# Hybrid decoder trunk on one core: retention's gated read-outs turned to channel rows by VectorE and a trip through DRAM on ScalarE's queue, in place of TensorE transposes

## The chip, the cores and the metric

One core of one Trainium2 chip. The time is device microseconds of the one program that the kernel launches; the median of three runs before the change is 1691.69 us. The core has five engines that run side by side, each with its own queue of instructions taken in order: TensorE (PE; PEld is its weight load), VectorE (DVE), ScalarE (ACT), GpSimd (POOL) and SyncE (SP), which only issues transfers. ACT and POOL issue transfers too, from the same queue as their computing. Engines wait for each other by semaphores; an instruction that waits holds all that stands behind it on its engine.

## The reference, cut to what matters

Two layers over 512 tokens of 1024 channels. Each layer mixes three branches of 512 channels (RWKV-7, retention, spatial gating), merges them by gates, and ends in a gated MLP. Of retention and the merge:

```python
y = (inner + cross).transpose(0, 2, 3, 1, 4).reshape(B, S, RET_HEADS, RET_V_DIM)
y = y * lax.rsqrt(jnp.mean(y * y, axis=-1, keepdims=True) + EPS)
return (y.reshape(B, S, RET_V_WIDTH) * jax.nn.silu(g)).astype(p.dtype)
...
branches = jnp.stack([y_rw, y_ret, y_sg], axis=2)
proj = jnp.einsum('bsgc,gcd->bsgd', branches, w_branch[l])
gates = jax.nn.sigmoid(gate_logits.reshape(B, S, N_BRANCH, D_MODEL))
x = x + jnp.sum(gates * proj, axis=2) @ w_out[l]
```

Retention has 4 heads with 128 value channels. Everything is float32 for the output's sake: a float32 product is made of three faster ones, with each operand split into a rounded high half and the low rest.

## The kernel before, in words

**Layout.** The merge wants a branch's output with channels on the partitions (128 channels by 512 tokens, one such tile per head). Retention is computed with tokens on the partitions: four chunks of 128 tokens, each a tile of 128 tokens by 512 channels, `yg[c]` (the trace and the order call these tiles vt). So `yg` has to be turned.

**Split products.** `mm3` (L157 inside it) makes one 128x128 by 128x512 product as three matmuls: low by high, high by high, high by low. `split` (L149, L150) makes the halves of an operand: a cast on ACT, then the difference on DVE. Weights go the same way: `load` (L127) brings 128x512 from DRAM on SP into one of three slots (wr), `part` (L140, L141) makes sh on ACT and sl on DVE. `unit` runs this ahead: in this stage, parts are written in the program three units before they are used. A load slot is free again when DVE has made its low half.

**Merges.** `merge(l, br, m, y)` loads a gate tile (gth) by a POOL transfer (L1071), makes one accumulator tile (acc, one of four in PSUM) with twelve matmuls from one unit, and empties it on DVE (L1074). Branch 0 is RWKV, 1 retention, 2 gating. Branch 2 adds to branch 0's tile on POOL (L1077), branch 1 on DVE, after which the sum is split. A fifth accumulator has to wait until the first of the four is emptied.

**Retention.** `ret_heads` prepares, `ret_pair` (matmuls at L948) is called three times: scores and states; read-outs of chunks 0 and 1 with scores of 2 and 3; read-outs of chunks 2 and 3, called the last pair below. A read-out is copied by ACT (L972), squared (L991), summed on DVE (L993, L994: rss), raised to -1/2 on POOL (L996: rrr), and multiplied into `yg` on DVE (L999, four products of 128x128 per chunk). `ret_out` (L1006) then transposes 16 blocks of 128x128 on TensorE into four PSUM tiles (sm), which `split` empties.

**Gating.** `sgu_out` (L1059) makes one of four blocks: four products into one sm tile, then DVE and a split.

**The order.** The string SEQ sets in which order `mixer` writes these steps into the program: 0, 1, 2 a merge of that branch; S a `ret_pair`; G a `sgu_out`; U units of gating's first factor; H `ret_heads`; Y `ret_out`. A scheduler then places the instructions on the engines by its own estimate of when each is ready, except those that are handed to `keep_in_program_order`, which stay in the order written. While `self.keep` is set, loads and parts of weights are among them. The matmuls of a merge are not pinned, so the scheduler may begin a merge, leave it for another and come back.

Of the kernel before, what the change touches and what calls it, by code (L numbers as in the profile page):

```python
# [8 lines left out]
F32 = mybir.dt.float32  # L9
F32R = mybir.dt.float32r  # L10
# [3 lines left out]
ADD, SUB, MUL, POW, MAX = ALU.add, ALU.subtract, ALU.mult, ALU.pow, ALU.max  # L14
# [3 lines left out]
S = 512  # L18
NC = 4
# [6 lines left out]
KEPT = 6  # L26
PRE = {(0, "f", 2): 0, (0, "f", 4): 1, (0, "f", 6): 2, (0, "f", 8): 3, (0, "d", 0): 4, (0, "d", 1): 5, (0, "d", 2): 6, (0, "d", 3): 7,
       (0, "d", 4): 8, (0, "d", 5): 9, (0, "d", 6): 10}
SEQ = "0 H G G 0 S 0 U U S G 0 G 0 0 S 2 2 Y 0 0 2 1 2 1 2 1 2 1 2 1 2 1 1 1"
NRAW = 3  # L30
AHEAD = {None: 2, "p": 4, "r": 3, "f": 3, "u": 5, "q": 4}
DEEP = 6
# [20 lines left out]
class Emit:  # L53
# [357 lines left out]
    def mixer(self, l, nst):  # L411
        self.pool = None
        with self.tc.tile_pool(name=f"rw{l}", bufs=1) as rp:
            self.rwp = rp
            self.filler = self.fillers(l)
            st = self.rwkv(l, nst)
        for _ in self.filler:
            pass
        self.rp = self.tc.tile_pool(name=f"ff{l}", bufs=NFP)
        self.fp = self.rp.__enter__()  # L420
        self.gup, self.bs, self.ws = self.f(n="gup"), self.f((128, 4, 128), n="bs"), self.f((128, 4, 128), n="ws")
        with self.tc.high_priority():
            self.nc.sync.dma_start(self.gup, self.a["gup"][l])
        self.nc.sync.dma_start(self.bs.rearrange("p g i -> p (g i)"), self.a["sgb"][l:l + 1, :].to_broadcast([128, 512]))
        self.nc.sync.dma_start(self.ws, self.a["sgw"][l])
        self.pool = "f"
        sg, out = self.sgu_v(l), self.rwkv_out(l, *st)
        self.nc.vector.tensor_tensor(self.ws, self.ws, self.c("le").unsqueeze(1).to_broadcast([128, 4, 128]), op=MUL)
        self.qk = []
        for c in range(NC):  # L430
            self.qk.append(self.f(n="qkT"))
            self.turned(self.qk[c], self.f(n="qkt"), self.ro[c], self.nc.gpsimd)
        self.wsp = self.split(self.ws.rearrange("p g i -> p (g i)"), self.f)
        for step in (sg, sg, out, sg, out, sg, None, out, sg, out, sg):
            next(step) if step else self.sgu_bias()
        yrw, ysg, mg, out, m2 = self.yrw, [], [], [], 0
        self.pool = "r"
        rest = self.sgu_u(l, range(2, 4))
        rows = iter([((), (0, 1), (0, 1, 2)), ((0, 1), (2, 3)), ((2, 3),)])
        for step in SEQ.split():  # L440
            if step == "S":
                self.ret_pair(*next(rows))
            elif step == "G":
                ysg.append(self.sgu_out(len(ysg)))
            elif step == "H":
                self.ret_heads()
            elif step == "U":
                next(rest), next(rest)
            elif step == "Y":
                yret = self.ret_out()  # L450
            elif step == "0":
                mg.append(self.merge(l, 0, len(mg), yrw))
            elif step == "2":
                mg[m2] = self.merge(l, 2, m2, ysg, mg[m2])
                m2 += 1
            else:
                out.append(self.split(self.merge(l, 1, len(out), yret, mg[len(out)], self.nc.vector), self.f))
        return out
# [398 lines left out]
    def ret_proj(self, l):  # L857
        nc, V, A, a = self.nc, self.nc.vector, self.nc.scalar, self.a
        g, tabs = self.supK(l, 14), []
# [5 lines left out]
        try:  # L865
            next(g)
        except StopIteration as e:
            pss = e.value
        self.ro, self.vt, self.yg, self.R, self.sc = [], [], [], {}, {}
        qs = [self.u(n="qs") for _ in pss]  # L870
        for c, ps in enumerate(pss):
            A.activation(qs[c], ps, AF.Identity, scale=self.rsT[:, c:c + 1])
# [3 lines left out]
        for i, out in ((18, self.vt), (22, self.yg)):  # L876
            g = self.supK(l, i)
# [8 lines left out]
            for c, ps in enumerate(pss):  # L886
                t = self.u(n="vt")
# [52 lines left out]
    def ret_pair(self, read=(), score=(), state=()):  # L940
# [47 lines left out]
        for k, c in enumerate(read):  # L988
# [8 lines left out]
            for i in range(4):  # L997
                o = g[:, 128 * i:128 * i + 128]
                V.scalar_tensor_tensor(o, y[:, i, :], rr[:, i:i + 1], o, op0=MUL, op1=MUL)  # L999

    def ret_out(self):
        out = []
        for h in range(4):
            pt = self.sm()
            for c in range(NC):
                self.tc.keep_in_program_order(self.nc.tensor.transpose(pt[:, c * 128:c * 128 + 128], self.yg[c][:, h * 128:h * 128 + 128], self.c("ident")))  # L1006
            out.append(self.split(pt, self.f))
        return out


    def sgu_v(self, l):
# [470 lines left out]
```

## Time and profile before

| what | value |
| --- | --- |
| median of three runs | 1691.69 us (1690.4 to 1692.12) |
| the profiled execution | 1690.56 us |
| its span, first to last instruction | 1688.9 us |
| mean granted TensorE clock | 0.999 of full |
| merges of layer 1, start of the first and last emptying (L1074) | 367.6 to 457.0 us of the span |
| the same of layer 2 | 1211.8 to 1301.2 us |

The span is what the profile divides into shares; the profiled execution's own time has 1.7 us around it. A row of the timeline has start, length, engine, line, operation and tiles, and in brackets how long the engine idled before it and for whom. A group row has count, then busy time in all, mean ns of one, and the idle time before it with its releaser. The chain of waits follows the program back from its last instruction, so its pieces have no gaps that another piece doesn't explain. Matmuls overlap: each lasts some 0.39 us, but the next begins sooner.

### The profile page before, as it was taken

What the parts mean: (1) busy time and instruction counts of PE and PEld (TensorE: products, weight loads), DVE (VectorE), ACT (ScalarE), POOL (GpSimd) and SP (SyncE); (2) the same over time, 40 slices, a digit from 0 to 9 for tenths busy, and PEclk for the clock granted to TensorE, in tenths of its full rate; (3) what the DMA queues carried; (4) which work ended last, traced back from release to release, by engine and by line L of the source; (5) the groups of instructions that cost most, each with busy time, mean ns of one, the idle gap of its engine ahead of it and who ended that gap; (6) DMA issues with size and microseconds to landing.
All of it is one profiled execution on the core that took longest, in us unless ns stands there. A gap on an engine that the chain in (4) does not pass through costs nothing.

```text
span 1688.9 us, 27943 instructions
## 1 busy us (share of the span) xinstructions
PE 1680.4 (100%) x10247; PEld 1382.5 (82%) x10247; DVE 1216.6 (72%) x2115; ACT 793.7 (47%) x1365; POOL 261.2 (15%) x376
## 2 busy tenths in 40 slices
PE   9999999999999999999999999999999999999998
PEld 7888877888888888888888888778888888888887
DVE  7888745578669887655568888455786688887777
ACT  6563543554255444433346544335542544444555
POOL 1121000303301200003321210003032012220000
PEclk9999999999999999999999999999999999999999
DMA  5236553625544532147743265536254424443775
GB/s 183 88 110 207 178 176 96 189 85 171 184 150 144 194 124 94 62 146 264 251 146 97 91 208 186 176 99 187 86 173 157 156 94 144 144 141 113 245 241 177
DMA packets 143385, 260.01 MB, mean 154 GB/s; under 512 B 19440, under 2 KB 35440, under 8 KB 143248
## 3 DMA queue, kind: packets, MB, share of 16 engines
q1 hardware_dynamic: 117056, 188.41, 34.7%
q0 software_dynamic: 17552, 54.15, 9.7%
q10 hardware_dynamic: 8640, 15.67, 2.6%
q8 instruction: 80, 1.31, 0.3%
q14 instruction: 57, 0.47, 0.1%
HBM read 212.94 MB, written 45.22 MB: 153 GB/s over the span
## 4 chain that ended last, share of the span: by engine, by line
PE 98%; DVE 1%; ACT 0%; issue 0%; DMA 0%; DVEq 0%; ACTq 0%
PE acc L157 89%; PE sm L157 3%; PE sm L696 2%; PE sm L948 1%; PE sm L603 1%; PE sm L1059 0%; PE acc L359 0%; PE sm L566 0%; PE sm L565 0%; PE sm L1006 0%; DVE wl L141 0%; PE sm L850 0%; PE acc L319 0%; PE sm L841 0%; DMA wr<-wall 0%
## 5 line engine op out<-in xcount | busy, mean ns | idle before, releaser
L157 PE MATMUL acc<-lo,sh 128*128 128x512 f32 x1108 | 432.9, 391 | 0.0
L157 PE MATMUL acc<-hi,sh 128*128 128x512 f32 x1108 | 431.6, 390 | 0.0
L157 PE MATMUL acc<-hi,sl 128*128 128x512 f32 x1108 | 425.2, 390 | 0.0
L140 ACT CAST sh<-wr 128x512 fp32r<-128x512 f32 (+1 forms) x375 | 226.5, 614 | 305.3 <-PE acc L157 163.8
L141 DVE TENSOR_TENSOR sl<-wr,sh 128x512 fp32r<-128x512 f32 (+1 forms) x375 | 253.2, 684 | 95.9 <-ACT sh L140 71.5
L141 DVE TENSOR_TENSOR wl<-wr,wh 128x512 fp32r<-128x512 f32 x238 | 168.2, 710 | 139.9 <-ACT wh L140 136.0
L140 ACT CAST wh<-wr 128x512 fp32r<-128x512 f32 x238 | 146.8, 619 | 246.6 <-PE acc L157 166.2
L157 PEld LDWEIGHTS acc<-lo,sh 128*128 128x128 f32 x1108 | 208.1, 188 | 43.9 <-issue 0.9
L157 PEld LDWEIGHTS acc<-hi,sl 128*128 128x128 f32 x1108 | 208.1, 188 | 43.4 <-issue 0.2
L157 PEld LDWEIGHTS acc<-hi,sh 128*128 128x128 f32 x1108 | 208.2, 188 | 42.5
L157 PE MATMUL acc<-lo,wh 128*128 128x512 f32 x584 | 230.2, 394 | 0.0
L157 PE MATMUL acc<-hi,wl 128*128 128x512 f32 x584 | 228.2, 391 | 0.0
L157 PE MATMUL acc<-hi,wh 128*128 128x512 f32 x584 | 227.9, 390 | 0.0
L1125 ACT ACTIVATE cv<-fu,pc 128x512 f32<-128x512 f32 x88 | 71.7, 816 | 134.6 <-DVE fu L1123 134.6
L157 PEld LDWEIGHTS acc<-lo,wh 128*128 128x128 f32 x584 | 109.7, 188 | 23.7 <-DVE rwp L525 0.3
L157 PEld LDWEIGHTS acc<-hi,wl 128*128 128x128 f32 x584 | 109.7, 188 | 23.7 <-issue 0.9
L157 PEld LDWEIGHTS acc<-hi,wh 128*128 128x128 f32 x584 | 109.7, 188 | 22.2 <-issue 0.2
L157 PE MATMUL acc<-ah,sh 128*128 128x512 f32 x352 | 108.5, 389 | 0.0
L1126 DVE SCALAR_TENSOR_TENSOR cv<-fu,pc,cv 128x511 f32<-128x511 f32 x88 | 65.9, 750 | 34.5 <-ACT cv L1125 34.5
L157 PE MATMUL acc<-wl,hi 128*128 128x512 f32 x212 | 85.8, 405 | 0.0
L157 PE MATMUL acc<-wh,hi 128*128 128x512 f32 x212 | 82.6, 389 | 0.0
L157 PE MATMUL acc<-wh,lo 128*128 128x512 f32 x212 | 82.5, 389 | 0.0
(368 smaller groups left out, 2428.6 us busy)
## 6 DMA issues: line engine op xcount, KB each, us to landing
wr<-wall SPq DMA_DIRECT2D x480, 256.0 KB, 2.8
gd<-gth ACTq DMA_DIRECT2D x48, 256.0 KB, 3.2
gth<-gd POOLq DMA_DIRECT2D x48, 256.0 KB, 3.5
pre<-wdt POOLq DMA_DIRECT2D x44, 256.0 KB, 5.9
ts<-pre POOLq DMA_DIRECT2D x44, 256.0 KB, 2.6
wr<-ts SPq DMA_DIRECT2D x44, 256.0 KB, 3.9
wr<-wdn SPq DMA_DIRECT2D x40, 256.0 KB, 4.0
wr<-wdt SPq DMA_DIRECT2D x33, 256.0 KB, 4.0
```

The costliest lines, as they stand in the source:

```text
L140: self.kept(self.nc.scalar.copy(hi[:, :n], raw[:, :n]))
L141: self.kept(self.nc.vector.tensor_tensor(lo[:, :n], raw[:, :n], hi[:, :n], op=SUB))
L157: i = self.nc.tensor.matmul(*x, **y, **kw)
L603: i = T.matmul(pK[hv[1 - h], j, :], bk[hv[h], c, 1, :], x[hv[h], c, :], start=True, stop=True)
L696: po(T.matmul(o, l, r, start=start, stop=True, skip_group_check=True))
L948: po(T.matmul(o, lhsT, rhs, start=start, stop=stop, skip_group_check=True))
L1125: A.activation(t, u, AF.Identity, scale=self.p("cw2", j), bias=self.p("cb", j))
L1126: V.scalar_tensor_tensor(t[:, 1:], u[:, :511], self.p("cw1", j), t[:, 1:], op0=MUL, op1=ADD)
```

## The change

`ret_out` no longer uses TensorE. `ret_write` takes two chunks at a time: DVE transposes each 32x32 block of `yg[c]` (yt), ACT's queue writes it to DRAM (tr), and after the first `next` the same queue reads it back in four strided pieces per chunk (yF), so that channels lie on the partitions. `ret_out` then casts each chunk's four quarters on ACT (hi) and makes the differences on DVE (lo), into the same kind of tiles as before. All of this is kept in program order, and `self.keep` is set from the first w until the last Y. SEQ changes: w and W are the writes and the reads of two chunks, Y is now taken three times, the last two gating blocks stand next to each other ahead of the middle pair, and merges of branch 2 stand between the steps.

```diff
-SEQ = "0 H G G 0 S 0 U U S G 0 G 0 0 S 2 2 Y 0 0 2 1 2 1 2 1 2 1 2 1 2 1 1 1"
+SEQ = "0 H G G 0 S 0 U U G G 0 S 0 0 w S 2 W 2 0 0 Y w 2 W 2 Y 2 Y 2 1 2 1 2 1 1 1 1 1 1"
...
-        rest = self.sgu_u(l, range(2, 4))
+        rest, turn = self.sgu_u(l, range(2, 4)), self.ret_out()
...
             elif step == "Y":
-                yret = self.ret_out()
+                yret = next(turn)
+                self.keep = len(self.yt) < NC or self.yt[3] is not None
+            elif step == "w":
+                trip, self.keep = self.ret_write(), True
+                next(trip)
+            elif step == "W":
+                next(trip, None)
...
+    def ret_write(self):
+        V, A, po, tr = self.nc.vector, self.nc.scalar, self.tc.keep_in_program_order, []
+        for g in self.yg[len(self.yt):len(self.yt) + 2]:
+            t, d = self.f(n="yt"), self.dp.tile([128, 512], F32, name=self.nm("tr"))
+            po(V.transpose(t.rearrange("p (f j d) -> p j f d", j=4, d=32), g.rearrange("p (j f d) -> p j f d", j=4, d=32)))
+            po(A.dma_start(d, t))
+            tr.append(d)
+        yield
+        for d in tr:
+            o = self.f(n="yF")
+            for f in range(4):
+                po(A.dma_start(o[32 * f:32 * f + 32, :].rearrange("d (a x) -> d a x", a=4), d[:, f * 128:f * 128 + 128].rearrange("(a d) x -> d a x", d=32)))
+            self.yt.append(o)
+
     def ret_out(self):
-        out = []
-        for h in range(4):
-            pt = self.sm()
-            for c in range(NC):
-                self.tc.keep_in_program_order(self.nc.tensor.transpose(pt[:, c * 128:c * 128 + 128], self.yg[c][:, h * 128:h * 128 + 128], self.c("ident")))
-            out.append(self.split(pt, self.f))
-        return out
+        out = [(self.f(dt=F32R, n="hi"), self.f(dt=F32R, n="lo")) for _ in range(4)]
+        for c in range(NC):
+            y = self.yt[c].rearrange("p (a j d) -> p j a d", j=4, d=32)
+            for h in range(4):
+                hi, lo = [t[:, 128 * c:128 * c + 128].rearrange("p (a d) -> p a d", d=32) for t in out[h]]
+                self.tc.keep_in_program_order(self.nc.scalar.copy(hi, y[:, h]))
+                self.tc.keep_in_program_order(self.nc.vector.tensor_tensor(lo, y[:, h], hi, op=SUB))
+            self.yt[c] = None
+            if c:
+                yield out
```

(`self.yt` starts as an empty list in `ret_proj`.) What the scheduler makes of it is shown at three places of layer 1; layer 2 has the same pattern. The numbers in the names are buffers; lines are those of each kernel's own file.

**POOL, around the last pair.** rrr_887 and rrr_890 (before) and rrr_891 and rrr_894 (after) are the powers of the last pair's sums. Before:

```order
L1071 DMA gth_862_4428<-gd_321_1524 128x512
L1071 DMA gth_871_4462<-gd_330_1566 128x512
L1071 DMA gth_876_4484<-gd_339_1608 128x512
L1071 DMA gth_891_4552<-gd_438_2070 128x512
L1071 DMA gth_896_4575<-gd_448_2119 128x512
L996 TENSOR_TENSOR rrr_887_4535<-rss_886_4532,con_78 128x4
L1077 TENSOR_TENSOR gth_790_4136<-gth_790_4136,gth_891_4552 128x512
L996 TENSOR_TENSOR rrr_890_4546<-rss_889_4543,con_78 128x4
```

After:

```order
L1094 DMA gth_895_4560<-gd_438_2070 128x512
L1002 TENSOR_TENSOR rrr_891_4543<-rss_890_4540,con_78 128x4
L1094 DMA gth_902_4593<-gd_448_2119 128x512
L1094 DMA gth_907_4616<-gd_348_1650 128x512
L1094 DMA gth_912_4638<-gd_357_1692 128x512
L1100 TENSOR_TENSOR gth_790_4136<-gth_790_4136,gth_895_4560 128x512
L1002 TENSOR_TENSOR rrr_894_4554<-rss_893_4551,con_78 128x4
```

The gate of the second merge of branch 2 (gd_448) was loaded ahead of the first power and is now loaded behind it, with the two gates after it.

**DVE and TensorE, three merges behind the last pair.** acc_896, acc_903 and acc_908 are those three merges, sl_899 the low half of the weights of merge acc_913. VectorE after:

```order
L1097 SCALAR_TENSOR_TENSOR gth_895_4560<-gth_895_4560,acc_896_4562 128x512
L1000 TENSOR_SCALAR rss_893_4551<-rss_893_4551 128x4
L1005 SCALAR_TENSOR_TENSOR vt_681_3723<-ry_887_4532,rrr_891_4543,vt_681_3723 128x128 x4
L1097 SCALAR_TENSOR_TENSOR gth_902_4593<-gth_902_4593,acc_903_4595 128x512
L1097 SCALAR_TENSOR_TENSOR gth_907_4616<-gth_907_4616,acc_908_4618 128x512
L1005 SCALAR_TENSOR_TENSOR vt_683_3728<-ry_888_4535,rrr_894_4554,vt_683_3728 128x128 x4
L141 TENSOR_TENSOR sl_899_4566<-wr_873_4465,sh_898_4565 128x512
```

TensorE after, from the last matmul of acc_908:

```order
L157 MATMUL acc_908_4618<-hi_783_4121,sl_880_4490 128x512
L157 MATMUL acc_913_4640<-lo_764_4009,sh_898_4565 128x512
L157 MATMUL acc_913_4640<-hi_763_4008,sh_898_4565 128x512
L157 MATMUL acc_930_4694<-lo_805_4181,sh_905_4598 128x512
L157 MATMUL acc_930_4694<-hi_804_4180,sh_905_4598 128x512
L157 MATMUL acc_937_4727<-lo_805_4181,sh_910_4621 128x512
L157 MATMUL acc_937_4727<-hi_804_4180,sh_910_4621 128x512
L157 MATMUL acc_913_4640<-hi_763_4008,sl_899_4566 128x512
```

TensorE before, at the place of the first transposes:

```order
L157 MATMUL acc_897_4577<-hi_869_4458,sl_875_4468 128x512
L1006 MATMUL sm_901_4598<-con_78,vt_677_3713 128x128
L1006 MATMUL sm_901_4598<-con_78,vt_679_3718 128x128
L157 MATMUL acc_914_4636<-lo_764_4009,sh_879_4489 128x512
L157 MATMUL acc_914_4636<-hi_763_4008,sh_879_4489 128x512
```

Where the old order runs whole merges with transposes between, the new one begins three merges with two matmuls each before the third matmul of the first, which reads sl_899; behind it the merges run acc_913, acc_930, acc_937, acc_942, acc_947.

**ACT and TensorE, the second trip and the first merge of branch 1.** tr_926 and tr_928 are the trips of chunks 2 and 3, yF_934 and yF_935 what is read back; hi_917 and lo_918 are the halves of head 0, acc_952 the first merge of branch 1, acc_959 one of branch 2. ScalarE after:

```order
L1012 DMA tr_926_4685<-yt_925_4684 128x512
L1012 DMA tr_928_4689<-yt_927_4688 128x512
L140 CAST sh_932_4697<-wr_909_4619 128x512
L1018 DMA yF_934_4715<-tr_926_4685 32x4x128 x4
L1018 DMA yF_935_4720<-tr_928_4689 32x4x128 x4
L140 CAST sh_939_4730<-wr_914_4641 128x512
L1027 CAST hi_917_4660<-yF_934_4715 128x128
L1027 CAST hi_919_4662<-yF_934_4715 128x128
L1027 CAST hi_921_4664<-yF_934_4715 128x128
L1027 CAST hi_923_4666<-yF_934_4715 128x128
L140 CAST sh_944_4761<-wr_931_4695 128x512
L1027 CAST hi_917_4660<-yF_935_4720 128x128
```

TensorE after:

```order
L157 MATMUL acc_947_4789<-hi_850_4378,sl_933_4698 128x512
L157 MATMUL acc_952_4812<-lo_918_4661,sh_939_4730 128x512
L157 MATMUL acc_952_4812<-hi_917_4660,sh_939_4730 128x512
L157 MATMUL acc_952_4812<-hi_917_4660,sl_940_4731 128x512
L157 MATMUL acc_959_4839<-lo_805_4181,sh_944_4761 128x512
```

ScalarE before, the four casts in the place of all this:

```order
L140 CAST sh_950_4783<-wr_937_4731 128x512
L149 CAST hi_902_4603<-sm_901_4598 128x512
L149 CAST hi_905_4612<-sm_904_4607 128x512
L149 CAST hi_908_4621<-sm_907_4616 128x512
L149 CAST hi_911_4630<-sm_910_4625 128x512
L140 CAST sh_955_4806<-wr_942_4754 128x512
```

On ScalarE's queue, casts of weights now stand between the writes, the reads and the quarter casts of the trip. On TensorE the first three matmuls of acc_952, the first of which reads all four chunks of lo_918, stand ahead of acc_959. On VectorE the second trip's transposes (yt_925, yt_927) stand behind sl_916, the eviction of acc_913 and the eight differences of chunks 0 and 1.

2 lines of the change are left out of this document (1 added, 1 removed).

## The prediction, made before the changed kernel was run

> **What bounds the kernel now.** I read the page's busy shares and its chain first, then the chain of waits in the merge stage, then the rows of VectorE (DVE), ScalarE (ACT) and GpSimd (POOL) there.
>
> ```profile
> span 1688.9 us, 27943 instructions
> PE 1680.4 (100%) x10247; PEld 1382.5 (82%) x10247; DVE 1216.6 (72%) x2115; ACT 793.7 (47%) x1365; POOL 261.2 (15%) x376
> PEclk9999999999999999999999999999999999999999
> PE 98%; DVE 1%; ACT 0%; issue 0%; DMA 0%; DVEq 0%; ACTq 0%
> ```
>
> TensorE (PE) is the bound, at full granted clock: 98% of the chain is its own work. So a matmul that goes away shortens the program by its spacing, and a microsecond in which TensorE waits lengthens it by one. Everything else is paid only where it makes TensorE wait. The chain of waits in the merges (start, length, what):
>
> ```profile
> 354.57 2.72 PE acc L157 x12
> ...
> 367.49 1.78 PE sm L1059 x16
> ...
> 381.59 3.32 PE sm L948 x40
> ...
> 386.95 0.89 PE sm L1059 x8
> 387.84 0.92 PE acc L157 x4
> 388.76 0.89 PE sm L1059 x8
> ...
> 395.11 2.88 PE sm L948 x32
> 397.99 5.67 PE acc L157 x24
> 403.65 0.22 PE sm L1006 x2
> 403.87 3.91 PE acc L157 x17
> 407.78 0.11 PE sm L1006
> 407.89 2.30 PE acc L157 x10
> 410.19 1.42 PE sm L1006 x13
> ```
>
> One merge is twelve matmuls in 2.72 us, 0.227 each. No gap stands between the pieces, and the last two read-out pairs (381.59 and 395.11) are followed by merges at once. L1006 are the transposes that go: 0.22 + 0.11 + 1.42 = 1.75 us of TensorE. The group's count, 32, is 16 for each layer, so I count 1.75 twice:
>
> ```profile
> L1006 PE MATMUL sm<-con,vt 128*128 128x128 f32 x32 | 4.5, 272 | 0.0
> ```
>
> **The change, part by part.** *Removed:* 2 x 1.75 = 3.5 us of TensorE, all on the chain. The four casts and four differences that emptied the transposes' PSUM tiles lay beside it: nothing.
>
> *The gating blocks in a pair:* 16 matmuls in a row took 1.78 us, 8 alone 0.89 twice: nothing.
>
> *Added* per layer: four block transposes, four writes to DRAM and 16 reads back, 16 quarter casts and 16 quarter differences. None is on TensorE. Each is paid only if the first merge of branch 1, or something queued behind it, is late. The prices, from groups (count | busy, mean ns), the DMA table (KB, us to landing) and the DMA rows of two tiles (issue min/median/max in ns):
>
> ```profile
> L140 ACT CAST sh<-wr 128x512 fp32r<-128x512 f32 x367 | 223.5, 618 | 290.8 <-PE acc L157 163.8 <-DMA wr<-wall 50.2 <-DMA wr<-wdn 40.4
> L141 DVE TENSOR_TENSOR sl<-wr,sh 128x512 fp32r<-128x512 f32 x367 | 249.9, 690 | 95.9 <-ACT sh L140 71.5 <-PE acc L157 14.1 <-issue 7.9
> L1074 DVE SCALAR_TENSOR_TENSOR gth<-gth,acc 128x512 f32<-128x512 f32 x48 | 32.1, 682 | 0.1
> L1077 POOL TENSOR_TENSOR gth<-gth,gth 128x512 f32<-128x512 f32 x16 | 21.4, 1338 | 54.1 <-DVE gth L1074 54.1
> L236 DVE STREAM_TRANSPOSE yt<-y 128x512 f32<-128x512 f32 x8 | 5.6, 697 | 0.0
> ```
> ```profile
> wr<-wall SPq DMA_DIRECT2D x480, 256.0 KB, 2.8
> gth<-gd POOLq DMA_DIRECT2D x48, 256.0 KB, 3.5
> tr<-yt SPq DMA_DIRECT2D x8, 256.0 KB, 3.0
> yF<-tr SPq DMA_DIRECT2D x32, 64.0 KB, 2.0
> ```
> ```profile
> L479 ACTq DMA_DIRECT2D gd<-gth x48: 326/332/377, 101.7 to 1086.9; - x48
> L239 SPq DMA_DIRECT2D yF<-tr x32: 325/424/523, 245.7 to 1163.9; - x32
> DMA to landing us min/median/max: 2.0/3.0/7.4
> ```
>
> (The last line belongs to tile yt.) And the rows of the old order that time the read-outs:
>
> ```profile
> 400.55 0.69 DVE L993 TENSOR_REDUCE rss<-rsq 128x4 f32<-128x512 f32 x1 [0.33 <-ACT rsq L991]
> 391.58 1.14 DVE L999 SCALAR_TENSOR_TENSOR vt<-ry,rrr,vt 128x128 f32<-128x128 f32 x4
> 389.27 1.13 DVE L999 SCALAR_TENSOR_TENSOR vt<-ry,rrr,vt 128x128 f32<-128x128 f32 x4
> 403.71 2.19 DVE L999 SCALAR_TENSOR_TENSOR vt<-ry,rrr,vt 128x128 f32<-128x128 f32 x4
> 390.19 2.71 POOL L1071 DMA_DIRECT2D gth<-gd  x5
> 402.66 1.02 POOL L996 TENSOR_TENSOR rrr<-rss,con 128x4 f32<-128x4 f32 x1 [9.75 <-DVE rss L994]
> 346.39 1.65 ACT L780 ACTIVATE yF<-yF,pc 128x128 f32<-128x128 f32 x4
> 398.80 1.19 ACT L972 COPY ry<-sm 128x256 f32<-128x256 f32 x4
> ```
>
> What is new lies in three waits.
>
> *First wait, behind POOL's queue.* The old order issued five gate loads together at 390.19, 4.9 us before the last read-out pair. The new one puts the load of gth_902 behind rrr_891, the power of that pair's own sums, and on VectorE the eviction that needs this load stands ahead of sl_899, the low half of the weights of merge acc_913. Counted from the start of the last pair: the reduction begins at 400.55 - 395.11 = 5.4 us (the trip's first writes now stand on ScalarE ahead of the pair's copies and wait for the transposes of the middle pair: that pair's last product ended 11.1 us after its start, 391.58 + 1.14 - 381.59, and with 1.4 for transposes and without the two gating blocks between, some 2.8 of VectorE work, it is near 10; the middle pair starts 2 merges and 3.3, 8.8 us, earlier, so they are done about 1 to 2 us in, before the pair's own 2.88 are over). Two reductions and a small row, 1.5: 6.9. Power 1.02: 7.9. Gate load 3.5: 11.4. Two evictions of 0.68: 12.8. Four products, 1.13 when alone and 2.19 beside a busy POOL: 13.9 to 15.0. sl_899, 0.69: 14.6 to 15.7. TensorE by then has the pair (2.88), three merges (8.16) and the six matmuls that the order gives it ahead (1.36): 12.4. It waits **2.2 to 3.3 us; I take 2.7**, the middle, since POOL has an add and loads to do there for part of the time.
>
> *Second wait, the trip.* From TensorE's restart, when sl_899 has also freed a load slot: the next weights load 2.8, their cast 0.62 and difference 0.69: 4.1. Eviction 0.68: 4.8. Eight quarter differences of chunks 0 and 1 stand ahead of the second trip's transposes. The trace has no such quarter: 0.28 each by the four products in 1.13, up to 0.55 by those in 2.19; I take 0.28, the plainer operation: 7.0. Two transposes of 0.70; the first ends at 7.7, and its write lands 3.0 later at 10.7. Eight reads on ScalarE's queue, 0.33 each by its own row, 0.42 by that of the same reads on SP's; I take 0.42, the same shape: 14.1. The last lands 2.0 later, beside what follows. One cast, 14.7. Four quarter casts: 0.41 each by the four in 1.65 (same quarter, strided too), 0.15 by half of the four half-tiles in 1.19; I take 0.41: 16.4. One cast and one quarter, 17.4; its difference with hand-over, 17.8. That is the earliest at which merge acc_952, first of branch 1, can start, and on TensorE it stands ahead of merge acc_959, which needs none of this. TensorE meanwhile has 30 matmuls of the three opened merges (6.8) and two merges (5.44): 12.2. It waits **about 5.5 us**. With the shortest write (2.0), reads of 0.33 and quarters of 0.15 it is 2.4; with the slowest write of the row (7.4), 9.9; one such write in eight makes 8 the end for the range.
>
> *Third wait, catching up.* Later evictions stand behind gate loads that follow POOL's adds: eviction 0.68, add 1.34, load 3.5 make 5.5 us for two merges of 5.44. Nothing is to spare, so lateness is kept, and an accumulator that isn't emptied holds the merge four places on. The trace has no row for it: nothing at best, one add and one eviction (2.0) in two such rounds, 4, at worst. I take 2.5, above the middle, since 5.5 is over 5.44.
>
> Per layer 2.7 + 5.5 + 2.5 - 1.75 = 8.95 us, so 17.9 for two. The profiled execution took 1690.56 us, its span of 1688.9 and 1.7 around it; 1.1 more is the median of the runs, 1691.69. So 1690.6 + 17.9 = 1708.5 for that execution, **1709.6** for the median.
>
> **The rivals.**
>
> *The trips fit (other side).* TensorE never waits and the transposes are saved: 1691.7 - 3.5 = 1688.2. For it: ScalarE is 47% busy, and in the old trace its casts wait mostly for TensorE. It decides at one point: the last quarter difference must be done within 12.2 us of the restart, and I count 17.8. Chance 0.06.
>
> *Only the shortest trip.* POOL's power comes early enough, the first wait and the third are gone, and the second is its lower bound: (2.4 - 1.75) x 2 = 1.3, so 1693.0, which is no change. Against it: the power can't precede the reductions that it needs. Chance 0.06.
>
> *Weights starve too.* Cast sh_932 now stands on ScalarE behind the two writes, which wait for the second transposes: 8.4 + 2 x 0.33 + 0.62 + 0.69 = 10.4 for its difference, and TensorE wants it at 6.8 + 2.72 = 9.5. About 1 us per layer more: 1711.6. For it: the sum itself. Against: the wait may only come out of the second. Chance 0.10.
>
> *The clock falls after the long wait.* If TensorE came back at half pace for one merge after 5.5 idle us, 2.72 more per layer: 1715.0. The trace's granted clock is full in all 40 slices and it has no such gap, so the rows say neither way. Chance 0.15. [...]
>
> That the change does not do what it says is ruled out by the order of its instructions: no transpose of that line is left on TensorE.
>
> **How the numbers follow.** The forecast has 0.63. Its own ends: 2.2 + 2.4 + 0 - 1.75 = 2.85 per layer, 1697.4; 3.3 + 8 + 4 - 1.75 = 13.55, 1718.8. The starved and the clock rival lie inside. The two quick rivals below, 0.12, and some 0.06 above are left out: 1697 to 1719. A measurement tells 0.2%, 3.4 us, from no change; the first rival lies at -3.5 (faster 0.06), the second at +1.3 (same 0.06), all else is slower (0.88).
>
> **What would show it.** Right: no L1006-like rows on TensorE and 16 fewer small matmuls in each layer's merges; a gap on TensorE of 2 to 3 us shortly after the third merge behind the last pair, ended by VectorE's low half of weights; a gap of some 5 us ahead of branch 1's first merge, ended by a quarter difference; reads of the trip at about 0.4 us each on ScalarE's queue; VectorE waiting for POOL's gate load before the first gap. Wrong: no gap ahead of branch 1; trips that land before the seventh merge of branch 2 ends; a first gap without a late gate load; clock below full in that slice speaks for the fourth rival.

## The result and the profile after

The median is 1723.01 us (five runs, 1720.92 to 1724.24) beside 1691.69 us before (five runs, 1690.4 to 1696.0): a ratio of 1.0182, 95% interval 1.017 to 1.0194, 31.3 us slower. 1709.6 was forecast, with a range to 1719. The page of the changed kernel:

```profile
span 1721.7 us, 28024 instructions
PE 1689.2 (98%) x10215; PEld 1383.2 (80%) x10215; DVE 1227.7 (71%) x2147; ACT 795.6 (46%) x1389; POOL 260.8 (15%) x376
PEclk9999999999999999999999999999998999999999
PE 90%; DMA 3%; DVE 3%; ACT 1%; issue 1%; ACTq 0%; SPq 0%; DVEq 0%; POOL 0%; POOLq 0%
```

TensorE's share of the chain fell from 98% to 90%, DMA and DVE rose from 0 and 1% to 3% each, and one of the 40 slices no longer has the full clock. TensorE's waits, by line and releaser (total us, times, longest):

```profile
PE acc L157 <- DVE lo L1028: 13.6, 2, 7.1
PE acc L157 <- DVE gth L1097: 5.7, 4, 1.9
PE acc L157 <- DVE sl L141: 3.8, 3, 1.8
```

L1028 is a quarter difference, the end of the trip; L141 the low half of weights; L1097 the emptying of an accumulator. In time, from TensorE's timeline of both layers:

```profile
411.35 0.50 PE L157 MATMUL acc<-hi,sl 128*128 128x512 f32 x1 [1.76 <-DVE sl L141]
...
431.22 0.79 PE L157 MATMUL acc<-lo,sh 128*128 128x512 f32 x1 [7.10 <-DVE lo L1028]
431.81 0.63 PE L157 MATMUL acc<-hi,sh 128*128 128x512 f32 x1
432.24 0.63 PE L157 MATMUL acc<-hi,sl 128*128 128x512 f32 x1
...
448.40 0.47 PE L157 MATMUL acc<-lo,sh 128*128 128x512 f32 x1 [1.69 <-DVE gth L1097]
...
464.23 0.47 PE L157 MATMUL acc<-lo,sh 128*128 128x512 f32 x1 [1.94 <-DVE gth L1097]
...
1272.55 0.50 PE L157 MATMUL acc<-hi,sl 128*128 128x512 f32 x1 [1.71 <-DVE sl L141]
...
1292.17 0.79 PE L157 MATMUL acc<-lo,sh 128*128 128x512 f32 x1 [6.46 <-DVE lo L1028]
```

Both layers have the first wait, the long second one, and two waits on emptyings in branch 1's merges (the shortest, 0.16 us, is not among the lines). Behind the second, matmuls last 0.63 us and start 0.43 apart in place of 0.227: TensorE runs at half pace. The windows show it (stretch, its length, busy time of PE, PEld, DVE, ACT, POOL with counts, then the granted clock, DMA share, GB/s):

```profile
410.30:413.72 3.42, 2.37 (x10) 1.98 (x11) 2.20 (x5) 0.00 (x0) 0.00 (x0) 1.00 0.64 172
427.37:430.78 3.41, 0.00 (x0) 0.00 (x0) 2.40 (x7) 2.04 (x9) 1.41 (x1) 0.50 0.73 158
430.78:434.20 3.42, 2.98 (x7) 2.40 (x8) 3.42 (x7) 1.92 (x5) 2.19 (x4) 0.50 0.24 77
461.51:464.92 3.41, 1.47 (x7) 0.95 (x6) 2.66 (x4) 1.26 (x3) 0.17 (x1) 1.00 0.98 324
464.92:468.34 3.42, 3.42 (x10) 2.64 (x9) 1.98 (x3) 0.54 (x1) 0.00 (x0) 0.50 0.25 92
1290.94:1294.35 3.41, 2.18 (x5) 1.80 (x6) 2.58 (x6) 2.55 (x7) 2.18 (x2) 0.50 0.27 90
1294.35:1297.77 3.42, 3.42 (x9) 2.65 (x9) 1.87 (x3) 0.00 (x0) 1.15 (x3) 0.50 0.56 177
1325.07:1328.48 3.41, 3.41 (x10) 2.62 (x9) 2.12 (x4) 0.62 (x1) 0.00 (x0) 0.50 0.22 72
```

**Where 32.8 us of span went.** Waits: 13.6 + 5.7 + 3.8 = 23.1. They are counted from the end of a matmul, 0.39 after its start, where the next would have begun after 0.227; nine waits add 9 x 0.16 = 1.4. Half clock: half of the busy time in the slow windows, (2.98 + 3.42 + 2.18 + 3.42 + 3.41) / 2 = 7.7. Transposes: -3.5. Sum 28.7. Measured between the same products, the two layers from the merges on are 15.1 and 13.9 us longer, 29.0. The other 3.8 lie outside, where the code is the same: 1.9 before the first merges, a point that the kernels profiled here reach anywhere from 352.7 to 355.2 us, and 1.9 between the first layer's end and the second's merges, a stretch that took them 337.2 to 339.5 us. So it is spread between executions.

### The profile page after: what moved, and what is told of

Its sections match the earlier page's. It is cut to its first block, busy times and chain, and to the rows that moved or that the text cites. A ratio compares the mean times of both kernels' runs of the same rounds, so it can differ in the third digit from the quotient of the medians.

```text
span 1721.7 us, 28024 instructions
## 1 busy us (share of the span) xinstructions
PE 1689.2 (98%) x10215; PEld 1383.2 (80%) x10215; DVE 1227.7 (71%) x2147; ACT 795.6 (46%) x1389; POOL 260.8 (15%) x376
## 4 chain that ended last, share of the span: by engine, by line
PE 90%; DMA 3%; DVE 3%; ACT 1%; issue 1%; ACTq 0%; SPq 0%; DVEq 0%; POOL 0%; POOLq 0%
PE acc L157 81%; PE sm L157 3%; PE sm L702 2%; DMA wr<-wall 2%; PE sm L954 1%; DMA yF<-tr 1%; PE sm L609 1%; DVE sl L141 1%; ACT sh L140 0%; PE sm L1082 0%; DMA wua<-wua 0%; DVE wl L141 0%; ACTq L1018 0%; DMA bkS<-tr 0%; PE acc L359 0%
## 5 line engine op out<-in xcount | busy, mean ns | idle before, releaser
L157 PE MATMUL acc<-lo,sh 128*128 128x512 f32 x1108 | 436.1, 394 | 19.4 <-DVE lo L1028 13.6
L141 DVE TENSOR_TENSOR sl<-wr,sh 128x512 fp32r<-128x512 f32 (+1 forms) x375 | 256.0, 693 | 98.1 <-ACT sh L140 74.9
L141 DVE TENSOR_TENSOR wl<-wr,wh 128x512 fp32r<-128x512 f32 x238 | 168.5, 711 | 144.7 <-ACT wh L140 141.8
```

The source lines that it names most:

```text
L141: self.kept(self.nc.vector.tensor_tensor(lo[:, :n], raw[:, :n], hi[:, :n], op=SUB))
L157: i = self.nc.tensor.matmul(*x, **y, **kw)
```

## The experiments

Each starts from the changed kernel unless it says otherwise. "Second wait" is the one ahead of branch 1's first merge; two numbers are layers 1 and 2. In the changed kernel it is 7.10 and 6.79 us (6.46 and a 0.33 shortly before it). Waits and clocks are those of one profiled execution. Times are medians, ratios are to the kernel before on the same chip; its median lay between 1690.6 and 1691.7 us on the chips used, so a difference between medians of two chips is good to about 1 us.

| run | median us | ratio, 95% interval |
| --- | --- | --- |
| e1 pairing alone | 1690.6 | 0.9997 (0.9987 to 1.0006) |
| e2 branch 1 later | 1729.1 | 1.022 (1.0203 to 1.0237) |
| e3 gap filled | 1719.1 | 1.0159 (1.0143 to 1.0176) |
| e4 gates early | 1719.2 | 1.0166 (1.0151 to 1.0181) |
| e5 late quarters, gates early | 1728.1 | 1.0217 (1.0202 to 1.0232) |
| e6 tail without additions | 1716.4 | 1.0151 (1.0134 to 1.0168) |
| e7 no gate loads beside the trip | 1717.4 | 1.0159 (1.014 to 1.0178) |
| e9 half trip | 1700.3 | 1.0051 (1.0038 to 1.0064) |
| e10 writes first | 1723.2 | 1.0186 (1.017 to 1.0201) |
| e11 gates early, writes first | 1715.9 | 1.0147 (1.0133 to 1.0161) |
| e12 and split late | 1708.1 | 1.0101 (1.0087 to 1.0115) |
| e13 one read in place of four | 1714.3 | 1.0138 (1.0125 to 1.0152) |
| e14 half trip, mended | 1694.6 | 1.0024 (1.0015 to 1.0033) |
| e15 half trip, one merge more | 1689.9 | 0.9992 (0.9983 to 1.0001) |
| e16 full trip, mended | 1701.9 | 1.007 (1.0053 to 1.0087) |

**e1, the pairing alone** (the kernel before, SEQ only).

```diff
-... U U S G 0 G 0 0 S 2 2 Y 0 0 2 1 ...
+... U U G G 0 S 0 0 S 2 2 Y 0 0 2 1 ...
```

> The kernel before with one part of the change alone: the last two gating blocks in one pair ahead of the middle read-out pair, transposes still on TensorE, no trips. Theory: the pairing is worth nothing, the whole 31 us come from the trips and from what their steps push aside: 1690 to 1693, no TensorE gap over 0.3 us in the merges. Rival: pulling the middle read-out pair 1 merge later and the pairing cost something by themselves: 3 us or more above the kernel before.

No gap, same time: the pair is worth nothing, as predicted.

**e3, the clock.**

```diff
+        for _ in range(26 * on):
+            self.tc.keep_in_program_order(self.nc.tensor.matmul(pf, x[:, 0:128], x, start=True, stop=True))
```

> The changed kernel with 26 extra matmuls (128x128 by 128x512, 0.227 us each, 5.9 us in all) into an unused PSUM tile, in TensorE's order between the last merge of branch 2 that is ready and the first merge of branch 1; the result is not touched. Theory: the clock falls because TensorE idles, so with the extra matmuls the clock stays full after the wait while the wait itself ends at the same time: some 1.5 and 2.7 us less in the two layers, 1718 to 1720. Rival: the slow matmuls come from something else (operands that arrive late): same time, slow matmuls still there. Rival: DVE is the bound behind the wait and takes it back in later gaps: clock full, time same.

The edit also fixes the order of the matmuls in the merge ahead of the extra ones and in the merge behind them. 3.9 us less, mean clock 0.999. The extra matmuls run during the wait, and the first product of branch 1 follows at full pace (TensorE's timeline):

```profile
423.90 6.05 PE L1024 MATMUL sm<-hi 128*128 128x512 f32 x26
...
431.23 0.50 PE L157 MATMUL acc<-lo,sh 128*128 128x512 f32 x1 [1.28 <-DVE lo L1033]
```

It starts at the same 431.2 us as without them, so the wait is as long; the slow matmuls behind it are gone. It was the idling that cost the clock: with the wait filled it is 1.00 in every window from 421.08 to 434.70, where the changed kernel has 0.50 from 427.37 to 434.20.

**e8, the clock by itself** (no layer; 96 bursts of matmuls with eight lengths of gap).

> No layer at all, only a measurement: 96 bursts of 30 to 46 matmuls (128x128 by 128x512), between them ScalarE copies that TensorE waits for, eight lengths of gap from under 1 to some 5 us, twelve of each at changing phase; the output is an input tile. Theory A, a free-running window of about 3.4 us, in which idling for more than some half of it makes the next window slow: gaps over 3.4 us always cost slow matmuls, gaps of 1.7 to 3.4 us sometimes, depending on where they fall, shorter ones never; slow stretches end on a grid of 3.4 us. [...]

The clock changes 106 times, each within 0.02 us of a grid with a period of 3.413 us that runs through the whole execution (mean clock 0.898). Sorted by idle time in one window of the grid: behind a full-clock window with up to 1.91 us of idling the next kept the clock (228 windows, beside the first of the execution, before any matmul); from 1.94 us on the next was slow (all 53). Behind a slow window with 0.56 us of idling or less the clock was full again (53), from 0.67 us on the next was slow too (20). The rows at the two edges, each pair a window and the next (PE, PEld, ACT, POOL, clock):

```profile
632.81:636.22 3.41, 1.50 (x7) 0.92 (x5) 1.75 (x3) 0.00 (x0) 1.00 0.00 0
636.22:639.64 3.42, 1.84 (x8) 1.54 (x9) 1.44 (x3) 0.00 (x0) 1.00 0.00 0
...
1175.53:1178.94 3.41, 1.47 (x7) 0.89 (x5) 1.81 (x4) 0.00 (x0) 1.00 0.00 0
1178.94:1182.36 3.42, 2.38 (x6) 1.90 (x7) 0.95 (x2) 0.00 (x0) 0.50 0.02 5
```

So theory A's grid holds in this run, and the edge, some half of a window in the theory, lies between 1.91 and 1.94 us of 3.413. The changed kernel's slow windows lie on a grid of the same period: its clock falls at 427.37, 464.92, 1290.94 and 1325.07 us, which are 11, 242 and 10 periods apart. Its tail gap of 1.94 us fell within one window and cost 1.7 us (461.51 and 464.92 above); the first wait of 1.76 is split by the grid at 410.30 and cost nothing. In e7 below, first waits of 1.76 and 1.79 us each fell within one window, and the next window was slow, though e8 kept the clock after 1.91. In layer 1 of e7:

```profile
408.05:411.46 3.41, 1.65 (x8) 1.23 (x7) 3.05 (x7) 0.00 (x0) 0.84 (x2) 1.00 0.41 108
411.46:414.88 3.42, 3.42 (x10) 2.68 (x9) 1.27 (x3) 1.92 (x8) 0.00 (x0) 0.50 0.64 203
```

**e4, the first wait.**

```diff
+                if len(mg) == 6:
+                    self.early = {(b, m): self.gate(b, m) for b, m in ((2, 0), (2, 1), (0, 6), (0, 7))}
                 self.ret_pair(*next(rows))
```

> The changed kernel with the four gate loads of the merges behind the last read-out pair issued ahead of that pair's powers on POOL's queue. Theory: the first wait (1.9 us in each layer) is the gate load behind the power: it falls to 0.3 or less, and the trip that starts from the same point on VectorE comes earlier by as much, so the second wait keeps its length: 3.5 us less, 1719. Rival: products and low half stand late on VectorE whatever the gate does: first wait stays above 1.2. Rival: the trip does not move with it: second wait grows by what the first loses, time same.

The first wait falls from 1.76 and 1.71 to 0.28 and 0.12: the gate load behind the power was the cause. The second stays in layer 1 (6.86) and grows by 1.3 us in layer 2 (0.27 + 7.86). In all 3.8 us less.

**e7, traffic beside the trip.**

```diff
+        if (br, m) in ((2, 3), (2, 4), (2, 5), (1, 0)):
+            g = self.g1
+        else:
+            nc.gpsimd.dma_start(t, self.gd[br, m])
```

> The changed kernel without the four gate loads that GpSimd issues while the second trip's reads are under way (256 KB each; the four merges take a gate tile that was loaded earlier, so their gates are not the reference's). Theory: the reads land 6.2 to 6.9 us after their issue, against 2.7 in the median, because those loads share the DMA engines: without them the reads land in 3 or less and the second wait falls from 7.3 and 6.6 to about 4; 6 to 10 us less with the clock, 1713 to 1717. Rival: landing is late by the reads' own pattern: second wait unchanged, 1722 to 1724. Part of a gain can come from GpSimd's queue being free of the loads, which would show in the first and later gaps and not in the landing.

The second wait falls to 4.07 and 4.29, 5.6 us less. In the changed kernel the DMA engines were full while the last reads were under way (DMA share is the last but one number):

```profile
424.00:430.00 6.00, 0.12 (x1) 0.00 (x0) 4.50 (x8) 2.03 (x6) 1.88 (x2) 0.78 0.98 267
```

In e7 the last read of layer 1 landed 2.18 us after its issue, in place of the 6.18 of the changed kernel (e7's chain of waits):

```profile
422.55 2.18 DMA yF<-tr
```

The eight reads landed after 1.9 to 3.4 us, median 2.8, in place of 1.9 to 6.9, median 5.8. So the landing was late because of the loads. The wait fell by less than the landing did; e10 below shows what else holds it. GpSimd's queue is freer in e7 too; what that alone is worth was not tried.

**e13, the issues.**

```diff
-            for f in range(4):
-                po(A.dma_start(o[32 * f:32 * f + 32, :].rearrange(...), d[:, f * 128:f * 128 + 128].rearrange(...)))
+            po(A.dma_start(o, d))
```

> The changed kernel with each chunk read back by one transfer of 256 KB in place of four strided ones of 64 KB: as many bytes, a quarter of the issues (the quarters are left in the order in which they lie in DRAM, so branch 1 gets permuted channels). The prediction's sum has eight reads at 0.42 us on ScalarE's queue, 3.4 us of the second wait. Theory: the issues are on the path, so the second wait falls by 2 to 3 us in each layer, 1715 to 1718. Rival: beside the gate loads the transfers themselves are the limit (the last read landed 6.2 us after its issue), so issuing earlier only makes them land as late: second wait less than 1 us shorter, 1721 to 1724.

The second wait is 4.45 and 4.10, 2.7 less in each layer with the same bytes. In layer 1 the issues took 1.00 us in place of 3.83, and the slowest read still landed 5.3 us after its issue (6.9): the issues are on the path too. A part may come from the other shape of the transfer, which was not tried alone. The total, 8.8 us less, is more than expected, since the first wait also shrank, to 1.08 and 1.07; the first trip has fewer issues on ScalarE too, but that this is why was not tried alone.

**e10, writes first.**

```diff
-... 0 0 Y w 2 W 2 Y ...
+... 0 0 w Y 2 W 2 Y ...
```

> The changed kernel with the second trip's block transposes and writes in the program ahead of the first trip's quarter casts and differences, nothing else. The prediction's sum has eight quarter differences (2.24 us at its 0.28 each) ahead of the second trip's transposes. Theory: this part of the second wait is in VectorE's and ScalarE's order, so the second wait falls by 2 to 3.4 us in each layer: 1716 to 1719. Rival: the trip then starts into more of the gate loads' traffic, its landing takes up the gain: second wait unchanged, 1722 to 1724.

My theory fell: 7.15 and 8.62. The trip did come earlier (its last quarter cast began at 425 us, not 430), but VectorE could not use it (its timeline):

```profile
419.53 0.68 DVE L1097 SCALAR_TENSOR_TENSOR gth<-gth,acc 128x512 f32<-128x512 f32 x1
423.66 0.69 DVE L141 TENSOR_TENSOR sl<-wr,sh 128x512 fp32r<-128x512 f32 x1 [3.45 <-ACT sh L140]
424.27 0.68 DVE L1097 SCALAR_TENSOR_TENSOR gth<-gth,acc 128x512 f32<-128x512 f32 x1
424.87 1.98 DVE L1028 TENSOR_TENSOR lo<-yF,hi 128x128 fp32r<-128x128 f32 x4
```

VectorE stands 3.45 us for a weight cast that is queued on ScalarE behind the eight reads (3.71 us of issues). Then the four differences take 0.50 us each, not 0.28, with GpSimd adding beside them (425.03, 1.27 us). So the second wait has two paths of nearly one length, the trip's landing and VectorE behind ScalarE's queue; shortening one leaves the other.

**e6, the tail.**

```diff
-        if sum is None:
+        if sum is None or br == 1 and m > 1:
             return t
```

> The changed kernel without the additions to the sum in the last six merges of branch 1 on VectorE (0.69 us each; the output lacks branches 0 and 2 in those six tiles). The prediction had the late gaps from the chain eviction, GpSimd addition, gate load. Theory now: they come from VectorE's own queue, where addition, difference of the sum's halves and low half of the weights stand ahead of the eviction that TensorE waits for: without the additions the gaps of 1.9 and 2.1 us in layer 1 and 2.1 in layer 2 go to under 1.2, and the slow matmuls behind the last one with them: 6 to 10 us less, 1713 to 1717. By the chain over GpSimd nothing changes in those gaps: 1722 to 1724.

6.6 us less: the 1.94 us gap in each layer is gone, with its slow window, but one of 1.57 stays in layer 1. So VectorE's queue, not GpSimd's chain, made the last gap. How, the changed kernel's VectorE shows:

```profile
460.68 0.68 DVE L1100 TENSOR_TENSOR gth<-gth,gth 128x512 f32<-128x512 f32 x1
462.11 0.69 DVE L150 TENSOR_TENSOR lo<-gth,hi 128x512 fp32r<-128x512 f32 x1 [0.74 <-ACT hi L149]
462.79 0.69 DVE L141 TENSOR_TENSOR sl<-wr,sh 128x512 fp32r<-128x512 f32 x1
463.40 0.68 DVE L1097 SCALAR_TENSOR_TENSOR gth<-gth,acc 128x512 f32<-128x512 f32 x1
```

The emptying at 463.40, for which TensorE waits, stands behind a difference that waits for ScalarE's cast of the sum before it.

**e2 and e5, the order alone.**

```diff
-... Y w 2 W 2 Y 2 Y 2 1 2 1 2 1 1 1 1 1 1
+... Y w 2 W 2 Y 2 Y 2 2 2 1 1 1 1 1 1 1 1     (e2)
+... w Y 2 W 2 2 2 2 Y Y 2 1 1 1 1 1 1 1 1     (e5, with e4's gates)
```

> The changed kernel with the last two merges of branch 2 moved ahead of the first merge of branch 1 (all eight merges of branch 1 in a row at the end). Theory A, only the first merge of branch 1 waits for the trip: two merges (5.44) cover that much of the gaps of 7.3 and 6.6, what is left is 1.8 and 1.2 us, no half clock behind it: some 14 us less, 1709. Theory B, the weights of those merges are held too, because their casts stand on ScalarE's queue behind quarter casts that wait for the trip: the gap only falls to about 5, the clock still drops behind it: 4 us less, 1719. More gaps in the tail of eight merges of branch 1, 2 us each, would take some of it back.

> The changed kernel with the early gate loads of e4 and the steps of the read-outs in another order: the second trip's writes ahead of the first trip's quarters, the quarters of the last two chunks behind six and not four merges of branch 2, merges of branch 1 all at the end. Theory: both waits are a matter of the order, so with the trip started 3.4 us earlier (eight casts and differences no longer ahead of it) and 5.4 us more cover the first merge of branch 1 no longer waits; what is left are the gaps in the tail of branch 1 (up to 2 us each, three to four in a layer, with a slow stretch): 1700 to 1708. Rival: the trip's reads land so late beside gate and weight loads that the gap stays above 3: 1712 or more. Rival: all gaps go, 1688.

Both are slower than the change, and both missed their forecast. In e2 the one gap breaks up into waits for weights, as theory B had it (6.1 us for casts and 1.7 of the 5.5 for low halves; the other 3.8 are the first waits), and eight merges of branch 1 in a row bring six waits on emptyings:

```profile
PE acc L157 <- DVE gth L1097: 15.2, 6, 4.4
PE acc L157 <- ACT sh L140: 6.1, 3, 3.7
PE acc L157 <- DVE sl L141: 5.5, 5, 2.0
```

In e5 the quarter differences still hold TensorE 2.58 and 1.28 us, late weight casts up to 2.70, and the tail has seven gaps of 1.1 to 4.2. I had foreseen 1700 to 1708: moving merges alone did not help.

**e11 and e12, remedies together.** e11 has e10's order and e4's early loads, for nine gates in place of four. e12 also writes each split one merge of branch 1 later:

```diff
-                out.append(self.split(self.merge(l, 1, len(out), yret, mg[len(out)], self.nc.vector), self.f))
+                late.append(self.merge(l, 1, len(late), yret, mg[len(late)], self.nc.vector))
+                if len(late) - len(out) > 1:
+                    out.append(self.split(late[len(out)], self.f))
```

> The changed kernel with the three remedies together: gate loads of nine merges issued ahead of the last pair's powers (so none runs beside the second trip), and the second trip's writes ahead of the quarters. If the parts add up: first wait 0, second 7.3 - 3.0 - 2.7, some 1.5 us, no half clock behind it; the gaps in the tail of branch 1 stay: 1700 to 1706. If the tail's gaps grow as TensorE comes earlier: 1706 to 1712. Rival: the second wait is held by something else (weights behind the trip on ScalarE's queue): over 4 us left, 1712 or more.

> e11 with the split of each sum written one merge of branch 1 later, so that VectorE's queue can have the next eviction ahead of the difference that waits for ScalarE. Theory of the tail (addition, difference and low half ahead of the eviction on VectorE): the gaps of 2.1 us near the end of branch 1 fall under 1 and the slow matmuls behind them go: 4 to 8 us below e11. Rival, late weights are what holds the tail: same as e11.

e11 missed: the second wait is 3.69 and 3.48 and the tail's gaps stay. e12 is 7.8 us below it and has no wait on an emptying left (e11's row was 6.1 us, four times), as its theory of the tail said:

```profile
PE acc L157 <- DVE lo L1033: 8.0, 2, 4.2
PE acc L157 <- DVE sl L141: 3.0, 3, 1.8
```

**e9, e14, e15, the half trip.** Two chunks go through DRAM, the last two are transposed on TensorE. e9 has the order of the kernel before. e14 takes the quarters ahead of the transposes, one merge more ahead of branch 1, and the late split; e15 one more merge. None of the three keeps loads and parts of weights in program order during the trip, as the changed kernel does.

```diff
+            for c in (2, 3):
+                self.tc.keep_in_program_order(self.nc.tensor.transpose(pt[:, c * 128:c * 128 + 128], ...))
...
+... w S 2 W 2 Y 0 0 2 1 2 1 2 1 2 1 2 1 2 1 1 1           (e9)
+... w S 2 W 2 Y Y 0 0 2 2 1 2 1 2 1 2 1 2 1 1 1 1         (e14)
+... w S 2 W 2 Y Y 0 0 2 2 2 1 2 1 2 1 2 1 1 1 1 1         (e15)
```

> A hybrid: only the first two chunks go through DRAM (written and read long before they are needed), the last two are still transposed on TensorE (8 matmuls of 128x128 in each layer in place of 16), in the order of the kernel before with the gating pair. Theory: the change loses by the second trip's latency alone; the first trip hides, so nothing waits and half of the transposes, 0.9 us in each layer, is saved: 1689 to 1690 beside 1691, a ratio of 0.999. Rival: the first trip's reads and quarter casts on ScalarE's queue hold weight casts too: a gap of 1 to 3 us in each layer, 1693 to 1698.

> The hybrid of e9 (first two chunks through DRAM, last two transposed on TensorE) with what the runs so far point to: the first trip's quarters ahead of the transposes, one more merge of branch 2 ahead of the first of branch 1, and the split of each sum one merge of branch 1 later. If order alone made e9 lose (its gaps of 2.9 and 4.7 us stood ahead of the first merge of branch 1): no gap over 0.5 us in the merges, 1688.5 to 1691, the first version not slower than the kernel before; at best 0.9 us in each layer are to be had, 0.1%. Rival: weight casts behind the first trip's reads on ScalarE's queue still hold TensorE once in each layer: 1693 to 1697.

> e14 with one more merge of branch 2 (2.72 us) ahead of the first merge of branch 1. e14's profile kept gaps of 0.7 and 2.4 us there. Theory: they are the last wait that the half trip causes, so they go and the 8 transposes saved in each layer show: 1688 to 1690, a ratio of 0.998 to 0.999. Rival: the row of five merges of branch 1 at the end brings a gap of 2.1 us back: 1692 to 1696.

e9 waits 2.77 and 4.62 us for quarters, e14 0.53 and 2.18, and both are slower than their theories had it (1690 and 1691 at most). The profile of e15, its shortest run, has no wait in the merges, and its time is the kernel before's or a little under it. The interval holds 1, so a gain is not shown; that half a trip costs nothing once nothing waits for it, is.

**e16, the full trip with its cover** (e12, with all eight merges of branch 2 ahead of branch 1 and the last quarters behind two merges more).

> e12 (all four chunks through DRAM, gates early, writes first, split late) with the two last merges of branch 2 moved ahead of branch 1 and the last quarters behind two merges more. e12 kept gaps of 4.4 and 4.0 us ahead of branch 1 and the half clock behind them. Theory: cover is all that is missing there, 5.4 us more of it ends those gaps and their slow matmuls; what is left is some 2 us in each layer behind the last pair: 1692 to 1698. Rival, as in e2: weight casts behind the trip's reads on ScalarE's queue hold the merges that were to be the cover, so gaps of 2 to 4 us come up one or two merges earlier or later: 1703 to 1710.

```profile
PE acc L157 <- DVE gth L1106: 4.2, 4, 1.9
PE acc L157 <- ACT sh L140: 3.0, 2, 2.1
PE acc L157 <- DVE sl L141: 2.5, 3, 1.3
```

No quarter difference holds TensorE any more, and the mean clock of this execution, the shortest of four, is 0.999. What is left, 9.7 us, is waits for weights and emptyings. 1701.9 lies between the theory's range and the rival's, nearer to the rival's: cover hides the trip's landing, but weights still come late. That the trip's reads and casts make them late is argued, not shown.

## Why the prediction was right or wrong, point by point

- **Bound, pair, transposes.** Right: TensorE bounds; the pair is worth nothing (e1); 32 transposes fewer in the page's count (10247 to 10215).
- **First wait, 2.2 to 3.3, taken 2.7.** Mechanism right (e4). Measured 1.76 and 1.71, 1 us less. In layer 1 the pair starts at 396.82: the reductions came 4.8 us behind it (5.4 in the sum), the low half was done after 14.5 (14.6 to 15.7), and TensorE's own work took 12.8 (12.4). The chain of waits shows power, load, products, low half in the forecast order:

```profile
403.17 0.51 POOL rrr L1002
...
404.73 3.83 DMA gth<-gd
...
408.66 0.21 DVE gth L1097
...
409.26 1.43 DVE vt L1005 x4
410.69 1.21 DVE sl L141 x2
```

- **Second wait, taken 5.5.** Place, releaser and path right, size short: 7.10, and 6.46 + 0.33 (a late low half 9 us ahead of it, all that came of "weights starve too"). From the restart at 411.35 I had the first product of branch 1 at 17.8 us; it came at 19.9. The first trip's differences ended 6.4 after the restart (7.0), the write took 2.05, not 3.0, and of the new operations, which the old trace did not have, the reads took 0.45, not 0.42, casts 0.29, not 0.41, differences 0.28 as taken (durations in ns, min/median/max):

```profile
L1018 ACTq DMA_DIRECT2D yF<-tr x32: 309/453/551, 401.1 to 1285.5; - x32
L1027 ACT CAST hi<-yF x32: 292/294/298, 414.8 to 1292.0; 128x128 fp32r<-128x128 f32 x32
L1028 DVE TENSOR_TENSOR lo<-yF,hi x32: 276/283/690, 416.1 to 1293.0; 128x128 fp32r<-128x128 f32 x32
```

All that made it earlier on the whole. The term that was mis-sized is "the last lands 2.0 later". The chain of waits from the write on:

```profile
418.44 2.05 DMA tr<-yt
...
423.94 6.18 DMA yF<-tr
...
430.15 0.90 ACT hi L1027 x4
```

6.18 us, because four gate loads of 256 KB, issued by GpSimd from 420.90 on, shared the engines; without them the last read lands after 2.18 us and the wait is 2.5 to 3.0 us shorter (e7). The forecast had these loads in view only as what a later eviction waits for, not as traffic beside the trip.

- **Rivals.** That the trips fit, or only their shortest form shows, fell with the second wait.
- **Third wait, 2.5 a layer.** Measured 3.63 and 2.10, so the mean of 2.9 came near by luck, for the reason was wrong: not the round of eviction, GpSimd addition and gate load, but VectorE's queue in a row of branch 1's merges (e6 and e12 for the gaps of 1.94). The gap of 1.69 in layer 1, which e6 leaves, stands behind VectorE's queue as well: the emptying at 447.58 comes behind a low half that waits 0.68 us for its cast, a difference and another low half.
- **The clock, given 0.15.** This is the step that failed most: the sum has nothing for it. The forecast kept the full clock since the old trace had no gap to judge by; the rival had half pace behind the long wait, and that came (clock 0.50 from 427.37 and from 1290.94 on), with its sign, a slice below full clock, in the page. Its 2.72 a layer, half pace for just one merge, was the author's estimate, and the old trace shows no such merge: the half clock behind the second wait was 1.5 and 2.8. A gap of 1.94 us in the tail of each layer cost 1.7 more, which neither foresaw: 3.2 and 4.5 a layer in all.

So two terms of the sum failed: the clock, put at nothing where 3.85 us a layer were measured, and the landing, 2.0 where it took 6.18, of which earlier parts of that wait took back all but 1.4.

Term by term, the mean of the layers: first wait -1.0, second +1.4, third +0.4, clock +3.85, the 0.16 us that each wait costs beyond its row +0.7: 5.4 a layer over the 8.95 forecast. The range ended at 1719 because its high end added the bounds of the three waits at full clock; "lie inside" was true of the rival with the waits as taken, not of the clock on top of longer waits. Without the 7.7 us of half clock the median would be some 1715.3, an estimate, inside the range.

## What to carry to other kernels

- The transfer that replaces work on the bound engine was paid here for what of its trip was not covered: issues on their queue (3.71 us for eight reads, e10), landing beside the other traffic of that moment (6.18 us, 2.18 without it, e7), and everything queued behind them (3.45 us of VectorE, e10). Half a trip with cover cost nothing (e15), and a whole one 11 us at best (e16).
- Read what the busy queues issue in the same microseconds before taking a median landing; and keep an accumulator's emptying ahead of anything on its queue that waits for another engine (e12: no wait on an emptying left, 7.8 us less).
- Price a gap on TensorE with the clock: where idling took 1.94 us or more of a window of 3.413 us (e8; 1.76 was enough in e7), the next window had half the clock, and a slow window full of matmuls cost 1.7 us, half its length (464.92 and 1325.07 in the changed kernel).

## What the hardware showed that was not expected

The granted clock changed on a grid with a period of 3.413 us that did not restart with the work: through all 96 bursts of e8, and over both layers of the changed kernel. In e8 1.94 us of idling or more in a full-clock window halved the clock of the next in every case (53), up to 1.91 in none (228); in the kernels' own traces the edge is blurred: a window with 1.76 us of idling halved the next (e7, from 408.05 on), one with 1.82 did not (the changed kernel, from 1284.12 on). The ends of matmuls are modelled in the profile, so this idle time may not be exactly what the clock goes by; what it counts stays open. Behind a slow window with 0.56 us of idling or less the clock was full again in e8, from 0.67 us on it was not. So a restart late in a window cost a second slow one: 1292.17 after 1290.94, with 1.23 us of that window idle, brought 5.6 us at half pace, 431.22 after 430.78, with 0.44 idle, 3.0. That one order of instructions can so differ from run to run, by where its gaps fall on the grid, fits e14, whose eleven runs spread from 1691.8 to 1697.5 us around gaps of 0.5 and 2.2, while e15, without them, spreads from 1687.8 to 1691.2. The mean clock was 0.999 in e14's three shortest runs and 0.998 in all the others; which windows these were can't be told, so this is argued, not shown.
